# Splitting a weight into hi and lo parts ahead of time and keeping both in DRAM: the second block's mixers

## The chip, the cores and the metric

The kernel runs on one core of a Trainium2 chip. A core has a matrix engine (PE in the profile), three engines for elementwise work (DVE is VectorE, ACT is ScalarE, POOL is GpSimd), a queue engine (SP) that issues this kernel's transfers, and 16 DMA engines that carry them between DRAM and the on-chip memory SBUF. Matrix products are summed in PSUM banks of 128 x 512 float32. The metric is the device time of one execution in microseconds; lower is better. Before the change the median of three runs is 2828.16 us (2825.42 to 2829.25).

## The reference, cut to what matters

Two transformer blocks run one after the other on 512 tokens (528 with 16 extra tokens in front in the first block), with model width 1024, all in float32.

- Block one has two hybrid layers. Each projects the normalized activations with `w_in`, runs three attentions (one with a forget gate, one with low-rank queries and keys, one with a sliding window), and ends with `merged = sum(sigmoid(gates) * (branches @ w_branch))` and `x + merged @ w_out`.
- Block two has two layers, each a mixer, an MLP `square(relu(h @ w_mlp_in)) @ w_mlp_out`, and a gated addition. Layer 0's mixer is `mixer_ab`: `h @ w_in_ab` feeds four differential-attention heads and eight dilated-attention heads, and their outputs are multiplied by `w_out_ab`. Layer 1's mixer is `mixer_c`: `h @ w_in_c` gives low-rank queries, keys and an index score; the 256 best keys of each query are selected; `w_qi`, `w_uq`, `w_uk`, `w_uv` make queries, keys and values, and `w_out_c` closes it.

The products must be close to float32 products. That is why every weight `w` and activation `a` is split in two: `w = hi + lo`, `a = hi + lo`.

## The kernel before, in words

Activations are held transposed, 128 channels to a tile and tokens along the free axis. Weights lie in DRAM in chunks of 128 output columns, each chunk `[128, kc, 128]` with `kc` groups of 128 input channels. A projection of one chunk (`proj`) is, for each of the `kc` groups, three matmuls into one PSUM bank: hi x hi, hi x lo, lo x hi.

`wload` brings a chunk in. It cuts it into pieces of 512 columns (four groups, at most 256 KB). For each piece SP issues a load into a raw tile (tag `wraw`, a ring of 4), ACT copies the raw tile to `wh` (line 383, this rounds it), and DVE or POOL subtracts to make `wl` (line 385). `wh` and `wl` are rings of 3 each, so a piece's buffers come free when PE has finished the matmuls of the piece three before. The engine of the subtraction goes round DVE, POOL, DVE (`weng`, counted by `wn`); while `mixer_c` selects its keys, `weng` holds POOL alone.

The order of work on each engine is set by a planner that simulates the program and places instructions by its own estimates of time; each engine and the SP queue then run their own list strictly in that order, so an instruction that waits holds up all that is queued behind it.

The stages that the change touches, in order of time:

- The end of a hybrid layer. A first loop over eight output chunks (`for oc in range(8)`, from `gate(2, oc, 1)`) loads three pieces for a gate and a branch and makes the merged activations. A second loop loads the two pieces of `wout`, and its consumer (lines 1177 to 1180 for layer 0, 1189 to 1192 for layer 1) loads a residual tile `xc` from DRAM, adds the product, stores it (`x1d` or `h2d`), and splits it for the next stage. Each layer's end has 16 iterations in all. The query tiles `s.qt` of the attentions (four hi/lo pairs) are no longer used there.
- `mixer_ab`, lines 1401 to 1531. Each of eight pairs of heads needs three chunks of `wab` (two pieces each, 48 pieces in all); a pair's rotary step sends four small transfers through SP (line 832). `out_part` with `woab` runs in three parts over the input channels (groups 0 to 3, 4 to 6, and 7), eight pieces in each, of four, three and one group: 24 pieces.
- The first MLP, `mlp` with `l = 0`: two halves of 16 input chunks (two pieces each) and eight output chunks (four pieces each).
- `mixer_c`, lines 1533 to 1746: `wc` has 14 pieces, `wqi` 8, `wuq2` 16, `wukv2` 8, and `woc` again 24: 70 pieces.

Of the kernel before, what the change touches and what calls it, by code (L numbers as in the profile page):

```python
# [10 lines left out]
F32 = mybir.dt.float32  # L11
F32R = mybir.dt.float32r
# [8 lines left out]
P = 128  # L21
KC = 8
NM = 16
NX = 512
# [7 lines left out]
RINGT = dict(tmp=4, mm=6, sm=2)  # L32
PLE1 = 4
AHEAD = 4
OUTK = 4, 7
MLA_SCALE = 96 ** -0.5
LAM_INIT = 0.8 - 0.6 * math.exp(-0.0)
# [250 lines left out]
class Kern:  # L288
    def __init__(s, ctx, tc, a, out):
        s.ctx, s.tc, s.nc, s.a, s.out = ctx, tc, tc.nc, a, out  # L290
        s.n = s.wn = 0
        s.weng = [tc.nc.vector, tc.nc.gpsimd, tc.nc.vector]

    def nm(s, x):
        s.n += 1
# [73 lines left out]
    def wload(s, src, pool=None):  # L369
        kc, n = src.shape[1], src.shape[2]  # L370
        nc = s.nc
        step = max(1, 512 // n)
        hs, ls = [], []
        for k0 in range(0, kc, step):
            m = min(step, kc - k0)
            raw = s.wp.tile([P, m, n], F32, tag="wraw", bufs=4, name=s.nm("wr"))
            nc.sync.dma_start(raw, src[:, k0:k0 + m])
            if pool is None:
                h = s.wp.tile([P, m, n], F32R, tag="wh", bufs=3, name=s.nm("wh"))
                l = s.wp.tile([P, m, n], F32R, tag="wl", bufs=3, name=s.nm("wl"))  # L380
            else:
                h, l = (pool.tile([P, NX], F32R, tag=x, name=s.nm(x)).rearrange("p (m n) -> p m n", m=m) for x in ("fh", "fl"))
            nc.scalar.copy(h, raw)  # L383
            s.wn += 1
            s.weng[s.wn % len(s.weng)].tensor_sub(l, raw, h.bitcast(F32))  # L385
            for k in range(m):
                hs.append(h[:, k])
                ls.append(l[:, k])
        return hs, ls

    def proj(s, w, acts, toks, c0=0, m=P, k0=0, tag="mm"):
# [447 lines left out]
    def hybrid(s, l, acts, rc, meta):  # L839

        nc, c = s.nc, s.c
# [5 lines left out]
        rstd = s.spread(rc, NT)  # L847
        win = s.a[f"win{l}"]
        W = lambda name: s.first.pop(name, None) or s.wload(win[WIN_IDX[name]])
        with ExitStack() as sc:  # L850
# [42 lines left out]
            for ps, t0, n in s.proj(W("misc"), acts, allt, tag="pv"):  # L893
# [3 lines left out]
            cq, rq = s.lora_raw([lambda i=i: s.proj(W(f"cq{i}"), acts, allt) for i in range(3)], f"cq{l}", ytile,  # L897
                                s.acc1(), NT, rc)
# [5 lines left out]
            for t0, n in allt:  # L904
                ps = s.bank("ax", "kf")
# [27 lines left out]
            ys = [[], [], []]  # L933
# [168 lines left out]
                       + [(swa, swa_do, swa_more, p) for p in range(4)])  # L1102
            yc = [ysplit(y) for y in ys[2]]
            mhl = []
            for oc in range(8):
                t = gate(2, oc, 1)
                branch(2, oc, yc, t, t)
                m = mg[oc]
                nc.gpsimd.tensor_add(m[:, c0:NT], m[:, c0:NT], t[:, c0:NT])
                h = s.yp.tile([P, NT], F32R, tag="y", name=s.nm("mh"))  # L1110
                lo = s.yp.tile([P, NT], F32R, tag="y", name=s.nm("ml"))
                nc.scalar.activation(h[:, c0:NT], m[:, c0:NT], AF.Copy, scale=0.5)
                nc.vector.scalar_tensor_tensor(lo[:, c0:NT], m[:, c0:NT], 0.5, h[:, c0:NT].bitcast(F32),
                                               op0=OP.mult, op1=OP.subtract)
                mhl.append((h, lo))

            for oc in range(8):
                w = s.wload(s.a[f"wout{l}"][oc])
                yield oc, s.proj(w, mhl, qt)

# [156 lines left out]
    def out_part(s, wname, acts, k0, k1, ys, tag=None, bufs=None):  # L1277

        acc = s.new_acc() if k1 == KC else None
        for oc in range(KC):  # L1280
            (ps, _, _), = s.proj(s.wload(s.a[wname][oc, :, k0:k1]), acts[k0:k1], [(0, NX)])
            if k0 == 0:
                y = s.t512(tag, bufs)
                s.nc.scalar.copy(y, ps)
                ys.append(y)
            else:
                s.nc.vector.tensor_add(ys[oc], ys[oc], ps)
            if k1 == KC:
                s.square_acc(ys[oc], acc, NX, oc == 0, oc == KC - 1)
        return ys, acc  # L1290
# [14 lines left out]
            s.nc.scalar.activation(t, ps, AF.Copy, scale=0.5)  # L1305
            s.pp.append(t)

    def mlp(s, l, acts, rstd, fp, w):
        nc = s.nc
        ys = []  # L1310
        acc = s.new_acc()
        r2 = s.tp.tile([P, NT], F32, tag="rstd", bufs=2, name=s.nm("r2"))
        nc.gpsimd.tensor_mul(r2[:, :NX], rstd[:, :NX], rstd[:, :NX])
        for half in range(2):
            ff = []
            for fc in range(16):
                (ps, _, _), = s.proj(w.pop(0) if w else s.wload(s.a[f"wmi{l}"][16 * half + fc]), acts, [(0, NX)])
                f = s.tmp("ff")[:, :NX]
                nc.vector.tensor_scalar(f, ps, 0.0, None, op0=OP.max)  # L1319
                nc.gpsimd.tensor_mul(f, f, f)  # L1320
                fh = fp.tile([P, NX], F32R, tag="fh", name=s.nm("fh"))
                fl = fp.tile([P, NX], F32R, tag="fl", name=s.nm("fl"))
                nc.scalar.copy(fh, f)
                nc.vector.tensor_sub(fl, f, fh.bitcast(F32))
                ff.append((fh, fl))
            for oc in range(KC):
                (ps, _, _), = s.proj(s.wload(s.a[f"wmo{l}"][oc, :, 16 * half:16 * half + 16]), ff, [(0, NX)])
                if half == 0:
                    y = s.t512("s", 16)
                    nc.scalar.copy(y, ps)  # L1330
                    ys.append(y)
                else:
                    y = ys[oc]
                    nc.vector.tensor_add(y, y, ps)
                    (nc.vector if oc == KC - 1 else nc.gpsimd).tensor_mul(y, y, r2[:, :NX])
                    s.square_acc(y, acc, NX, oc == 0, oc >= KC - 2)
        return ys, acc
# [19 lines left out]
    def tail_layer(s, l, ys, acc):  # L1357

        with ExitStack() as ps:
            s.rings(ps, **RINGT)  # L1360
            s.pp = []
            s.ple_proj(l, range(0, PLE1))
            with s.tc.tile_pool(name=f"ff{l}", bufs=16) as fp, s.tc.tile_pool(name=f"pe{l}", bufs=1) as pep:

                w = []
                acts, acc = s.post(ys, acc, f"mpost{l}", f"fpre{l}", lambda: w.extend(
                    s.wload(s.a[f"wmi{l}"][fc], fp) for fc in range(AHEAD)))
                rstd = s.rstd_of(acc, NX, 1024)
                s.ple_load(l, lambda: pep.tile([P, NX], F32R, name=s.nm("p")))
                ys, acc = s.mlp(l, acts, rstd, fp, w)  # L1370
                s.ple_proj(l, range(PLE1, KC))
            acts, _ = s.post(ys, acc, f"fpost{l}", None)
            sums = s.new_acc() if l == 0 else None
            s.ple_gate(l, acts, sums)
            return sums
# [25 lines left out]
    def mixer_ab(s, acts, rstd, load):  # L1401
# [4 lines left out]
        with ExitStack() as sc:  # L1406
# [21 lines left out]

            def scaled(ch, scale=1.0):
                v = s.tmp("v")  # L1430
                (ps, _, _), = s.proj(s.wload(s.a["wab"][ch]), acts, tk)
                nc.vector.scalar_tensor_tensor(v[:, :NX], ps, scale, rstd[:, :NX], op0=OP.mult, op1=OP.mult)  # L1432
                return v

# [98 lines left out]
    def mixer_c(s, acts, rc):  # L1533
# [4 lines left out]
        with ExitStack() as sc:  # L1538
# [6 lines left out]
            def raw(ch, n):  # L1545
                res = []
                for i in range(n):
                    v = s.t512("s", 16)
                    (ps, _, _), = s.proj(s.wload(s.a["wc"][ch + i]), acts, tk)
                    nc.vector.tensor_mul(v, ps, rstd[:, :NX])  # L1550
                    res.append(v)
                return res
# [4 lines left out]
            def lora(raw, gname):  # L1557
# [5 lines left out]
                for i, v in enumerate(raw):  # L1563
# [4 lines left out]
                    res.append((h, lo))  # L1568
                return res

            cq, rq = s.lora_raw([lambda i=i: s.proj(s.wload(s.a["wc"][2 + i]), acts, tk) for i in range(3)], "cq2", ctile,
                                s.new_acc(), NX, rc)

            (ps, _, _), = s.proj(s.wload(s.a["wc"][0]), acts, tk)
            s.table("kit", 0)
            s.table("qit", 1)
            foldki, selki = s.cld("foldki", kp), s.cld("selki", kp)
            kr = s.tmp("kr")[:, :NX]
            nc.vector.tensor_mul(kr, ps, rstd[:, :NX])
            nc.vector.tensor_mul(kr, kr, c["kit"][:, :NX])  # L1580
            (ps, _, _), = s.proj(s.wload(s.a["wc"][1]), acts, tk)
            m2 = s.tmp("m2")[:, :NX]
            nc.vector.tensor_mul(m2[0:64], ps[0:64], rstd[0:64, :NX])
            ps = s.bank("ax", "kf")
# [20 lines left out]
            score = [s.ap.tile([P, NX], F32, tag="Ph", bufs=3, name=s.nm("sc")) for _ in range(3)]  # L1605
            qi = []
            for h in range(8):
                (ps, _, _), = s.proj(s.wload(s.a["wqi"][h]), cq, [(P, 384)])
                q = s.tmp("qi")
                nc.vector.tensor_mul(q[:, P:NX], ps[:, :384], c["qit"][:, P:NX])  # L1610
                qh, ql = s.t512("s", 16, F32R), s.t512("s", 16, F32R)
                s.split(q[:, :NX], qh, ql, slice(P, NX), nc.vector if h % 2 else nc.gpsimd)
                qi.append((qh, ql))
# [20 lines left out]
            def query(i):  # L1634


                h, k = i & ~3, i & 3
                (ps, _, _), = s.proj(s.wload(s.a["wuq2"][i]), cq, tk)
                v = s.tmp("q")[:, :NX]
                if k < 2:  # L1640
                    for _ in range(2):
# [28 lines left out]
            outs = []  # L1670

            def mla(p):
                wkv = s.wload(s.a["wukv2"][p])
                v = s.tmp("v")
                (ps, _, _), = s.proj(wkv, ckv, tk, c0=P)
                nc.scalar.copy(v[:, :NX], ps)
# [88 lines left out]
```

## Time and profile before

| what | value |
|---|---|
| median of three runs | 2828.16 us |
| the profiled execution's own time | 2830.3 us |
| its span, first to last instruction | 2828.5 us |
| PE busy | 2708.7 us (96%) |
| DVE busy | 1629.7 us (58%) |
| ACT busy | 1225.3 us (43%) |
| POOL busy | 1186.1 us (42%) |
| mean granted TensorE clock | 0.978 of full speed |
| transfers on the SP queue | 249.43 MB, 29.5% of the 16 DMA engines' span |

The shares are averages over the whole span. PE is nearly always busy, but the profile's busy time counts a slowed matmul as fully busy, so the granted clock must be read beside it. What an engine's work is worth has to be read from its stage: DVE's share in particular is far from even over the span.

### The profile page before, as it was taken

To read this page: it belongs to the slowest core of one execution; us is meant where nothing else is said; L and a number is where in the kernel's file an instruction comes from. 1 tells how busy PE (TensorE), PEld (TensorE's weight loads), DVE (VectorE), ACT (ScalarE), POOL (GpSimd) and SP (SyncE) were. 2 spreads that over 40 slices of the span, in tenths; PEclk is the share of its full clock that TensorE was granted. 3 is DMA by queue.
4 is the path that set the end of the run, shared out by engine and by line. 5 is a ranking of instruction groups with operands and counts; after the bars stand their busy time and mean duration, and the time that the engine had idled before them with its cause. 6 is when DMAs were issued, how large, how long until landed. Compare 5 with 4: busy or idle time off the path is not lost. (4 is left out here: it accounts for less than half of the span.)

```text
span 2828.5 us, 41363 instructions
## 1 busy us (share of the span) xinstructions
PE 2708.7 (96%) x14962; PEld 2306.3 (82%) x14962; DVE 1629.7 (58%) x2997; ACT 1225.3 (43%) x2267; POOL 1186.1 (42%) x1091
## 2 busy tenths in 40 slices
PE   8999999999999999999988999999998898999998
PEld 7999999999888887877766768888776776788886
DVE  5666666644576667545688863132459876522325
ACT  4554444433454444434455543232344665322323
POOL 3455445432334334346455452133336434422333
PEclk9999999999999999999999999999999998999999
DMA  4222232234322233325322223333233212233322
GB/s 144 65 67 80 76 96 84 79 102 136 99 70 76 68 90 98 94 94 185 105 74 76 67 87 97 93 96 94 75 92 92 75 35 63 83 94 96 94 86 89
DMA packets 146669, 252.08 MB, mean 89 GB/s; under 512 B 19680, under 2 KB 32864, under 8 KB 146464
## 3 DMA queue, kind: packets, MB, share of 16 engines
q1 hardware_dynamic: 146464, 249.43, 29.5%
q8 instruction: 118, 1.93, 0.3%
q14 instruction: 87, 0.71, 0.1%
HBM read 215.26 MB, written 6.42 MB: 78 GB/s over the span
## 5 line engine op out<-in xcount | busy, mean ns | idle before, releaser
L383 ACT CAST wh<-wr 128x512 fp32r<-128x512 f32 (+3 forms) x774 | 463.8, 601 | 987.8 <-PE mm L362 815.8
L362 PE MATMUL mm<-xh,wh 128*128 128x264 f32 (+2 forms) x2464 | 849.4, 347 | 28.3 <-ACT xh L1141 8.2
L362 PE MATMUL mm<-xl,wh 128*128 128x264 f32 (+1 forms) x2480 | 852.0, 345 | 5.1 <-DVE xl L1142 1.7
L362 PE MATMUL mm<-xh,wl 128*128 128x264 f32 (+2 forms) x2464 | 845.4, 344 | 2.0 <-DVE wl L385 1.3
L385 POOL TENSOR_TENSOR wl<-wr,wh 128x512 fp32r<-128x512 f32 (+2 forms) x273 | 350.1, 1283 | 804.1 <-ACT wh L383 792.9
L385 DVE TENSOR_TENSOR wl<-wr,wh 128x512 fp32r<-128x512 f32 (+3 forms) x501 | 383.6, 766 | 398.6 <-ACT wh L383 389.9
L362 PEld LDWEIGHTS mm<-xh,wh 128*128 128x128 f32 x2464 | 469.8, 191 | 90.7 <-DVE v L1432 8.3
L362 PEld LDWEIGHTS mm<-xl,wh 128*128 128x128 f32 x2480 | 473.6, 191 | 62.2 <-DVE xl L1142 2.9
L362 PEld LDWEIGHTS mm<-xh,wl 128*128 128x128 f32 x2464 | 469.3, 191 | 58.9 <-DVE wl L385 3.2
L564 POOL TENSOR_TENSOR Pl<-P,Ph 128x512 fp32r<-128x512 f32 (+4 forms) x108 | 131.5, 1218 | 169.0 <-ACT P L563 144.9
L362 PE MATMUL mm<-fh,wl 128*128 128x512 f32 x512 | 202.3, 395 | 0.0
L362 PE MATMUL mm<-fl,wh 128*128 128x512 f32 x512 | 202.0, 395 | 0.0
L362 PE MATMUL mm<-fh,wh 128*128 128x512 f32 x512 | 202.0, 395 | 0.0
L563 ACT ACTIVATE Ph<-st 128x512 fp32r<-128x512 f32 (+4 forms) x224 | 122.1, 545 | 128.1 <-PE st L362 79.9
L564 DVE TENSOR_TENSOR Pl<-P,Ph 128x512 fp32r<-128x512 f32 (+4 forms) x108 | 83.1, 769 | 123.6 <-ACT P L563 110.7
L362 PE MATMUL mm<-c,wh 128*128 128x264 f32 (+2 forms) x480 | 127.9, 353 | 9.5 <-ACT q L1645 4.7
L1320 POOL TENSOR_TENSOR ff<-ff 128x512 f32<-128x512 f32 x64 | 82.2, 1286 | 106.3 <-DVE ff L1319 106.3
L701 DVE RECIPROCAL zr<-zr 128x128 f32<-128x128 f32 (+1 forms) x144 | 123.2, 916 | 2.7 <-ACT zr L710 2.4
L563 ACT ACTIVATE P<-st 128x512 f32<-128x512 f32 (+4 forms) x216 | 116.8, 541 | 6.5 <-POOL Pl L564 3.0
L483 POOL TENSOR_TENSOR acc<-acc,sq 128x512 f32<-128x512 f32 (+1 forms) x64 | 92.0, 1442 | 60.6 <-ACT sq L479 54.8
L362 PEld LDWEIGHTS mm<-fl,wh 128*128 128x128 f32 x512 | 96.5, 188 | 22.5
L362 PEld LDWEIGHTS mm<-fh,wl 128*128 128x128 f32 x512 | 96.5, 188 | 22.3
(612 smaller groups left out, 5154.2 us busy)
## 6 DMA issues: line engine op xcount, KB each, us to landing
wr<-in_win_dram SPq DMA_DIRECT2D x240, 256.0 KB
wr<-in_wmi_dram SPq DMA_DIRECT2D x128, 256.0 KB
wr<-in_wmo_dram SPq DMA_DIRECT2D x128, 256.0 KB
wr<-in_wbr_dram SPq DMA_DIRECT2D x48, 256.0 KB
wr<-in_wab_dram SPq DMA_DIRECT2D x48, 256.0 KB
wr<-in_wout_dram SPq DMA_DIRECT2D x32, 256.0 KB
wr<-in_wpg_dram SPq DMA_DIRECT2D x32, 256.0 KB
wr<-in_wuq_dram SPq DMA_DIRECT2D x32, 192.0 KB
```

The costliest lines, as they stand in the source:

```text
L362: s.nc.tensor.matmul(out, l, r, start=start, stop=stop)
L383: nc.scalar.copy(h, raw)
L385: s.weng[s.wn % len(s.weng)].tensor_sub(l, raw, h.bitcast(F32))
L483: e[eng[1]].tensor_add(sums.t[:, :T], sums.t[:, :T], q[:, :T])
L563: nc.scalar.activation(o[:, :col], ps[:, :col], AF.Exp)
L564: s.pl_eng(ui, hn).tensor_sub(pl[:, :col], p[:, :col], ph[:, :col].bitcast(F32))
L701: s.nc.vector.reciprocal(t[:, a:b], t[:, a:b])
L1320: nc.gpsimd.tensor_mul(f, f, f)
```

## The change

`pieces` lists a weight's pieces as keys. `ahead` takes the next keys from a list `todo`; for each it loads the raw piece, copies it to a hi tile, subtracts to a lo tile, and stores both tiles to a DRAM tile `d` of `[128, 2, w]`. `wget` takes the place of `wload` in the mixers: where a piece is found in `pre`, it loads hi and lo straight into `wh` and `wl` (two transfers, no ACT copy and no subtraction); otherwise it falls back to `wload`.

```diff
+AHEADN = (2, 2), (3, 2), (1, 3)
...
+    def ahead(s, count, tiles):
+        nc = s.nc
+        for _ in range(min(count, len(s.todo))):
+            key = name, ch, k0, m = s.todo.pop(0)
+            w = m * s.a[name].shape[3]
+            raw = s.wp.tile([P, m, w // m], F32, tag="wraw", bufs=4, name=s.nm("wr"))
+            nc.sync.dma_start(raw, s.a[name][ch, :, k0:k0 + m])
+            raw = raw.rearrange("p m n -> p (m n)")
+            d = s.dp.tile([P, 2, w], F32R, name=s.nm("wd"))
+            h, l = (t[:, :w] for t in tiles())
+            nc.scalar.copy(h, raw)
+            s.wn += 1
+            s.weng[s.wn % len(s.weng)].tensor_sub(l, raw, h.bitcast(F32))
+            s.rdma(d[:, 0], h)
+            s.rdma(d[:, 1], l)
+            s.pre[key] = d
+
+    def wget(s, name, ch, k0=0, k1=None):
+        hs, ls = [], []
+        for key in s.pieces(name, ch, k0, k1):
+            _, _, k, m = key
+            d = s.pre.get(key)
+            if d is None:
+                h, l = s.wload(s.a[name][ch, :, k:k + m])
...
+            h = s.wp.tile([P, m, n], F32R, tag="wh", bufs=3, name=s.nm("wh"))
+            l = s.wp.tile([P, m, n], F32R, tag="wl", bufs=3, name=s.nm("wl"))
+            for t, i in ((h, 0), (l, 1)):
+                s.rdma(t.rearrange("p m n -> p (m n)"), d[:, i])
...
             for oc in range(8):
+                s.ahead(AHEADN[l][0], tiles)
                 t = gate(2, oc, 1)
...
             for oc in range(8):
+                s.ahead(AHEADN[l][1], tiles)
                 w = s.wload(s.a[f"wout{l}"][oc])
...
             for fc in range(16):
+                if not w:
+                    later(AHEADN[2][0])
...
             for oc in range(KC):
+                later(AHEADN[2][1])
...
-                (ps, _, _), = s.proj(s.wload(s.a["wab"][ch]), acts, tk)
+                (ps, _, _), = s.proj(s.wget("wab", ch), acts, tk)
```

The same replacement of `wload` by `wget` is made for `woab` and `woc` (in `out_part`), `wc`, `wqi`, `wuq2` and `wukv2`. In the hybrid layers `tiles` hands out the four pairs of `s.qt` in turn; in the first MLP `later` uses a new pool with two hi and two lo tiles.

What is prepared where follows from the counts. The first `todo` (48 pieces of `wab`, 24 of `woab`) is used up in the two hybrid ends: 2 in each of 16 iterations of layer 0 (32 pieces), 3 and then 2 in each of eight iterations of layer 1 (40 pieces). The second (70 pieces) is used up in the first MLP: 1 in each of 28 input chunks, 3 in each output chunk.

## Rows read from the trace of the kernel before

**Rows 1.** The page: busy time of PE, and the granted clock in 40 slices.
```profile
PE 2708.7 (96%) x14962; PEld 2306.3 (82%) x14962; DVE 1629.7 (58%) x2997; ACT 1225.3 (43%) x2267; POOL 1186.1 (42%) x1091
...
PEclk9999999999999999999999999999999998999999
```

**Rows 2.** Stretches: stretch, length, busy us (instructions) of five engines, clock, DMA share, GB/s.
```profile
563.00:632.00 69.00, 67.25 (x550) 66.96 (x550) 32.55 (x59) 24.33 (x40) 26.52 (x18) 1.00 0.31 97
632.00:682.00 50.00, 50.00 (x414) 49.96 (x413) 22.70 (x38) 22.09 (x35) 18.16 (x13) 1.00 0.52 166
1205.00:1272.00 67.00, 67.00 (x290) 54.03 (x289) 30.82 (x43) 23.75 (x40) 26.42 (x20) 1.00 0.32 99
1272.00:1318.00 46.00, 46.00 (x216) 37.80 (x215) 20.41 (x34) 25.40 (x43) 31.54 (x35) 1.00 0.60 187
1340.00:1626.00 286.00, 255.84 (x1141) 196.99 (x1139) 233.17 (x396) 148.96 (x275) 146.56 (x120) 0.95 0.29 81
1672.00:2012.00 340.00, 340.00 (x1472) 275.21 (x1471) 102.00 (x150) 100.30 (x171) 108.28 (x84) 1.00 0.30 92
2075.00:2205.00 130.00, 114.05 (x517) 92.72 (x517) 102.49 (x231) 58.01 (x112) 66.36 (x56) 0.93 0.34 94
```

**Rows 3.** Waits of PE, 1318 to 1680 us: total us, times, longest.
```profile
PE mm L362 <- DVE v L1432: 5.9, 6, 1.5
PE st L362 <- DVE rz L1495: 4.9, 3, 2.8
...
PE zs L1479 <- POOL zacc L569: 3.6, 3, 1.6
...
PE sm L362 <- DVE ng L514: 2.7, 3, 1.4
```

**Rows 4.** Groups by line, 1340 to 1626 us: the weight split's three engines.
```profile
L385 DVE TENSOR_TENSOR wl<-wr,wh 128x512 fp32r<-128x512 f32 (+3 forms) x43 | 38.8, 903 | 4.1 <-ACT wh L383 3.8
L383 ACT CAST wh<-wr 128x512 fp32r<-128x512 f32 (+3 forms) x64 | 35.1, 555 | 40.2 <-PE mm L362 29.5 <-issue 8.3 <-ACT y L711 1.4
L385 POOL TENSOR_TENSOR wl<-wr,wh 128x512 fp32r<-128x512 f32 (+3 forms) x22 | 28.0, 1274 | 18.6 <-ACT wh L383 18.6
```

**Rows 5.** One line, 1340 to 1626 us: min/median/max ns.
```profile
L836 DVE TENSOR_TENSOR v<-v,sw x15: 674/1181/1778, 1341.9 to 1566.1; 128x512 f32<-128x512 f32 x15
```

**Rows 6.** A short stretch of the first mixer, columns as in rows 2.
```profile
1550.00:1556.00 6.00, 2.73 (x10) 1.59 (x9) 6.00 (x12) 4.19 (x8) 4.63 (x3) 0.73 0.22 72
```

**Rows 7.** The chain that ended last: start, us, what.
```profile
1545.78 1.97 DMA sw<-v
...
1572.76 2.77 PE mm L362 x12
...
1626.15 5.79 PE mm L362 x24
...
1636.79 2.71 DMA wr<-in_wmi_dram
...
2118.55 1.56 PE mm L362 x9
```

**Rows 8.** SP's queue in layer 0's last loop: start, us, instruction.
```profile
650.28 0.38 SPq L1180 DMA_DIRECT2D x1d<-xc  x1
650.71 0.42 SPq L1177 DMA_DIRECT2D xc<-in_xt_dram  x1
...
655.78 0.33 SPq L1180 DMA_DIRECT2D x1d<-xc  x1
```

**Rows 9.** The stretch with the highest transfer rate, columns as in rows 2.
```profile
10.00:14.00 4.00, 4.00 (x22) 3.79 (x20) 3.61 (x5) 4.00 (x8) 2.67 (x2) 1.00 1.05 402
```

**Rows 10.** The second mixer's key selection, columns as in rows 2.
```profile
2140.00:2145.00 5.00, 5.00 (x23) 4.05 (x22) 5.00 (x13) 2.24 (x5) 1.02 (x1) 1.00 0.07 25
2180.00:2185.00 5.00, 0.55 (x3) 0.13 (x1) 5.00 (x16) 0.51 (x1) 5.00 (x5) 0.93 0.38 89
```

**Rows 11.** POOL's groups by shape, 2100 to 2215 us.
```profile
L385 POOL TENSOR_TENSOR wl<-wr,wh 128x384 fp32r<-128x384 f32 x19 | 20.1, 1062 | 34.9 <-ACT wh L383 34.9
L385 POOL TENSOR_TENSOR wl<-wr,wh 128x512 fp32r<-128x512 f32 x6 | 7.9, 1314 | 4.8 <-ACT wh L383 4.8
```

More of the change, by code (lines that the diff above doesn't have):

```diff
@@ L292, in __init__ @@
         s.weng = [tc.nc.vector, tc.nc.gpsimd, tc.nc.vector]
+        s.pre, s.todo = {}, []
     def nm(s, x):
@@ L388, in wload, with pieces @@
                 ls.append(l[:, k])
+        return hs, ls
+    def pieces(s, name, ch, k0=0, k1=None):
+        kc, n = s.a[name].shape[2], s.a[name].shape[3]
+        k1 = kc if k1 is None else k1
+        step = max(1, 512 // n)
+        return [(name, ch, k, min(step, k1 - k)) for k in range(k0, k1, step)]
+    def ahead(s, count, tiles):
[21 more added lines that the diff above has]
+                h, l = s.wload(s.a[name][ch, :, k:k + m])
+                hs += h
+                ls += l
+                continue
+            n = s.a[name].shape[3]
+            h = s.wp.tile([P, m, n], F32R, tag="wh", bufs=3, name=s.nm("wh"))
+            l = s.wp.tile([P, m, n], F32R, tag="wl", bufs=3, name=s.nm("wl"))
+            for t, i in ((h, 0), (l, 1)):
+                s.rdma(t.rearrange("p m n -> p (m n)"), d[:, i])
+            for i in range(m):
+                hs.append(h[:, i])
+                ls.append(l[:, i])
         return hs, ls
@@ L1104, in hybrid, with tiles @@
             mhl = []
+            if l == 0:
+                s.todo = sum((s.pieces("wab", b + p) for b, q in ((0, 8), (12, 20)) for p in range(4)
+                              for b in ((q, b + 4, b))), [])
+                s.todo += sum((s.pieces("woab", oc, *r) for r in ((0, OUTK[0]), OUTK, (OUTK[1], KC)) for oc in range(8)), [])
+            turn = [0]
+            def tiles():
+                turn[0] += 1
+                return s.qt[turn[0] % len(s.qt)]
             for oc in range(8):
+                s.ahead(AHEADN[l][0], tiles)
                 t = gate(2, oc, 1)
@@ L1280, in out_part @@
         for oc in range(KC):
-            (ps, _, _), = s.proj(s.wload(s.a[wname][oc, :, k0:k1]), acts[k0:k1], [(0, NX)])
+            (ps, _, _), = s.proj(s.wget(wname, oc, k0, k1), acts[k0:k1], [(0, NX)])
             if k0 == 0:
@@ L1306, in ple_proj, with mlp, later @@
             s.pp.append(t)
-    def mlp(s, l, acts, rstd, fp, w):
+    def mlp(s, l, acts, rstd, fp, w, spare=None):
         nc = s.nc
         ys = []
+        if l == 0:
+            s.todo = sum((s.pieces("wc", ch) for ch in (2, 3, 4, 0, 1)), [])
+            for name, n in (("wqi", range(8)), ("wc", (5, 6)), ("wuq2", range(16)), ("wukv2", range(8))):
+                s.todo += sum((s.pieces(name, ch) for ch in n), [])
+            s.todo += sum((s.pieces("woc", oc, *r) for r in ((0, OUTK[0]), OUTK, (OUTK[1], KC)) for oc in range(8)), [])
+        def later(n):
+            if l == 0:
+                s.ahead(n, lambda: [spare.tile([P, NX], F32R, tag=x, bufs=2, name=s.nm(x)) for x in ("sh", "sl")])
         acc = s.new_acc()
@@ L1369, in tail_layer @@
                 s.ple_load(l, lambda: pep.tile([P, NX], F32R, name=s.nm("p")))
-                ys, acc = s.mlp(l, acts, rstd, fp, w)
+                with s.tc.tile_pool(name=f"sp{l}", bufs=1) as spare:
+                    ys, acc = s.mlp(l, acts, rstd, fp, w, spare)
                 s.ple_proj(l, range(PLE1, KC))
@@ L1548, in raw @@
                     v = s.t512("s", 16)
-                    (ps, _, _), = s.proj(s.wload(s.a["wc"][ch + i]), acts, tk)
+                    (ps, _, _), = s.proj(s.wget("wc", ch + i), acts, tk)
                     nc.vector.tensor_mul(v, ps, rstd[:, :NX])
@@ L1569, in lora @@
                 return res
-            cq, rq = s.lora_raw([lambda i=i: s.proj(s.wload(s.a["wc"][2 + i]), acts, tk) for i in range(3)], "cq2", ctile,
+            cq, rq = s.lora_raw([lambda i=i: s.proj(s.wget("wc", 2 + i), acts, tk) for i in range(3)], "cq2", ctile,
                                 s.new_acc(), NX, rc)
-            (ps, _, _), = s.proj(s.wload(s.a["wc"][0]), acts, tk)
+            (ps, _, _), = s.proj(s.wget("wc", 0), acts, tk)
             s.table("kit", 0)
@@ L1580, in mixer_c @@
             nc.vector.tensor_mul(kr, kr, c["kit"][:, :NX])
-            (ps, _, _), = s.proj(s.wload(s.a["wc"][1]), acts, tk)
+            (ps, _, _), = s.proj(s.wget("wc", 1), acts, tk)
             m2 = s.tmp("m2")[:, :NX]
@@ L1607, in mixer_c @@
             for h in range(8):
-                (ps, _, _), = s.proj(s.wload(s.a["wqi"][h]), cq, [(P, 384)])
+                (ps, _, _), = s.proj(s.wget("wqi", h), cq, [(P, 384)])
                 q = s.tmp("qi")
@@ L1637, in query @@
                 h, k = i & ~3, i & 3
-                (ps, _, _), = s.proj(s.wload(s.a["wuq2"][i]), cq, tk)
+                (ps, _, _), = s.proj(s.wget("wuq2", i), cq, tk)
                 v = s.tmp("q")[:, :NX]
@@ L1672, in mla @@
             def mla(p):
-                wkv = s.wload(s.a["wukv2"][p])
+                wkv = s.wget("wukv2", p)
                 v = s.tmp("v")
```

## The prediction, made before the changed kernel was run

> **What bounds the kernel now.** I read the page first, then a table of stretches by stage, then who PE waits for in the stretches that the change touches, and last the groups, the chain and the SP queue there. The page says that PE is busy 96% and its clock nearly full everywhere [rows 1], so this is a PE-bound kernel and an edit that takes work from other engines can only earn what PE idles or loses to its clock. Where that is shows in the stretches [rows 2]. The two hybrid ends (563 to 682 and 1205 to 1318 us) and the first MLP (1672 to 2012) have PE full, or all but 2 us of it, at clock 1.00: nothing can be won there, only lost. In the first mixer (1340 to 1626) PE is busy 255.84 of 286 us at clock 0.95, while DVE is busy 233.17, 82%. In the second mixer's first part (2075 to 2205) PE is busy 114.05 of 130.
>
> **What the change can win: first mixer.** Its ceiling is 286 - 255.84 = 30 us of idle PE, and (1 - 0.95) x 286 = 14 us of slow clock: 44 us. The clock belongs to the idle time: when PE was busy only 2.73 of 6 us with DVE full, the granted clock of that stretch fell to 0.73 [rows 6], between the levels of 2.4 and 1.2 GHz. The change takes from this stretch 43 DVE subtractions, 38.8 us, 22 on POOL, 28.0 us, and 64 ACT copies, 35.1 us [rows 4]; a few belong to the loads behind the mixer and stay. DVE falls to about 195 us, 68%. Its own slowed operations should gain too: one DVE addition took from 674 to 1778 ns at the same shape [rows 5], but I count nothing for that, since I can't say how many slow ones sit beside a subtraction that goes.
>
> How much of the 44 us comes back? PE's largest waits there are for DVE and POOL, 5.9 + 4.9 + 3.6 + 2.7 = 17.1 us [rows 3], and almost none is for a split weight itself. So what can be won is the queue in front of other DVE and POOL work. What is late next is the chain through a pair of heads: evacuation, rotary transfers, maxima, exponentials. I take 40% of the ceiling, 18 us: some 12 of idle time, two thirds of the named waits, and 6 of clock. Bounds: nothing (the chain is as long as before) and 36 us (80%).
>
> **What the mixers pay: loads that come late.** Before, a piece needs an ACT copy and a subtraction once its buffer is free: 0.55 + 0.90 us at the means on DVE, more with queues [rows 4]. Now SP must issue two loads when PE frees the buffer, at 0.33 to 0.42 us each [rows 8], and they land after 1.97 us (a small one) to 2.71 us (256 KB) [rows 7]: about 3.5 us. PE takes 2.77 us for twelve matmuls of a 512-column piece [rows 7], so two pieces in hand cover 5.5 us, and `wqi`'s pieces, 1.56 us each plus score matmuls [rows 7], cover a little over 3. Hidden, then, but with the cover thin, and the loads share SP with the rotary transfers: I put 1 us for it, from 0 to 8.
>
> The one-group pieces at the end of `woab` and `woc` have no such cover. Eight of them are 24 matmuls in 5.79 us, 0.72 each [rows 7]. Of the first three the loads go out while PE is still on larger pieces. The next three wait: free at 0.72, landed some 2.7 us later, done at about 5.6; the last two again, done near 8.3. That is 2.5 us more at each of the two mixer ends, on PE's path: 5 us, from 0 (casts and additions there are as slow) to 10.
>
> **Second mixer.** POOL loses 25 subtractions, 20.1 + 7.9 us [rows 11], in a stretch where it runs full at times. But DVE, which selects the keys, is full from 2140 on, also where PE has nearly nothing to do [rows 10], and subtractions there are POOL's already, so the end of the selection hardly moves. I take 3 us won, from 4 lost (the plan there changes) to 8 of the 16 us that PE idles.
>
> **What is added where PE is full.** The elementwise work first. In layer 0's last loop ACT, DVE and POOL are busy 22, 23 and 18 of 50 us [rows 2]; 16 copies and 16 subtractions at the means of rows 4 add 9 us to ACT and 14 to DVE, or 20 if all fell on POOL. It fits; cover gone, each would cost PE at most its length. The first MLP has a third of each engine busy in 340 us, and 70 pieces add 39 us to ACT and 63 to 89 us of subtractions: 0, at most 6 if copies wait for the two spare tiles.
>
> The transfers don't fit as well. A 256 KB piece now moves three times in these stages, read once and written twice: 0.786 MB. Layer 0's last loop takes 16 pieces, 12.6 MB, on top of 166 GB/s x 50 us = 8.3 MB: 418 GB/s would be wanted. The best that the trace shows is 402 [rows 9], so this loop is 2 us too short for its bytes. Layer 1's first loop takes 24 pieces on 99 GB/s: 381 GB/s; its last one 8 of 192 KB and 8 of 64 KB on 187 GB/s: 324; layer 0's first loop 279; the MLP's output half, 24 pieces of mostly 192 KB in about 88 us on 92 GB/s, some 265. The Trainium skill's page "HBM Reference", section "Specifications (TRN2)", gives an effective 358 GB/s per core, which speaks against this change; its text also lets a core that streams alone go well above that. Rows 9 have such a core at 402, so the measurement decides; by 358 the two stretches above it would be 8 and 4 us too short.
>
> Latency is the other half. In these loops SP stores a result, loads the next residual tile at 650.71, and the store that needs it follows at 655.78: 5.1 us in a period of 5.5 [rows 8]. Six more issues per iteration stand in this queue (2 raw loads, 4 stores that wait for copies and subtractions), 2 to 2.5 us at 0.33 to 0.42, and each raw load of a main weight and each residual tile waits behind up to 1.5 MB. Behind a waiting store stand the main weights; the rings hold some 8 us of those, PE's banks of results about one half-chunk. I take 5 us for layer 0 and 2 for layer 1, together 7, from 0 to 32 (2 us in each of 16 iterations).
>
> **Sum.** On the profiled execution's 2830.3 us, 2.1 above the median: -18 + 1 + 5 - 3 + 0 + 7 = -8, so 2822.3, and against the median of 2828.2 about 2820.
>
> **The rivals.**
> *The hybrid ends become bound by transfers.* From the point at which residual tiles and main weights land later than PE's banks allow, the loop's period is SP's and the queue's, not PE's. For it: 418 GB/s wanted where 402 was the best, and the 5.1 of 5.5 us. Against: weights run far ahead, and the other stretches stay below 402. The page named above belongs to this rival. Price: 1.75 us more in 16 iterations, 28 instead of 7: 2841.
> *The first mixer doesn't shorten.* The time per pair of heads is set by its chain, not by DVE's load, or the win goes to weights that wait behind rotary transfers. For it: waits for split weights were near nothing, and ring depth falls to three. Against: DVE at 82% with PE's waits naming it. Price: 7 won instead of 18, and the rest as above: 2831, near enough to no change.
> *The change doesn't do what it says.* All 72 and 70 pieces find their turn by the counts, so nothing falls back to the old path; I give it no chance of its own.
>
> **How the numbers follow.** Forecast 0.45, transfers bound 0.29, mixer unshortened 0.26. A measurement of this kernel can't tell less than 0.2%, 5.7 us, from no change. The forecast's own range is 2806 to 2824, so a little of it is no change, and the second rival reaches a bit to both sides: faster 0.46, same 0.24, slower 0.30. The time is the forecast's, 2820; the range takes both rivals in, 2798 to 2844.
>
> **What would show it.** After the change the first mixer's stretch should have no subtraction of mixer weights, DVE near 70%, and be 13 to 20 us shorter, with fewer low-clock stretches. PE should wait for loaded `wh` or `wl` in the one-group ends, some 2.5 us each, and hardly elsewhere. The hybrid ends should show 300 to 400 GB/s and PE idle a few us in layer 0's last loop. I am wrong if PE idles there by 20 us, if the first mixer is as long as before, or if the first MLP is no longer full.

## The result: 2.2% slower

The changed kernel takes 2890.0 us (median of 4 runs, 2878.41 to 2901.93) against 2827.2 us for the kernel before: ratio 1.0222, 95% interval [1.0202, 1.0241], or 63 us more. The forecast was 2820 and the range ended at 2844.

The page of the changed kernel: busy time, clock, the SP queue and the bytes.
```profile
PE 2728.3 (95%) x14962; PEld 2292.0 (80%) x14962; DVE 1650.8 (57%) x3012; ACT 1224.2 (43%) x2267; POOL 1167.0 (41%) x1076
...
PEclk9999999999999999999999999999999999999999
...
q1 hardware_dynamic: 228256, 375.30, 42.0%
...
HBM read 278.17 MB, written 69.34 MB: 121 GB/s over the span
```
Against [rows 1] PE does the same 14962 matmuls and its share falls. The SP queue carries 126 MB more, half of it stores. The profiled execution is the fastest of the four (2878.4 us, clock 0.984; the other three had 0.978 to 0.980), so the stages below add up to 48 of the 63 us.

The stretches that answer to [rows 2], in the same order: stretch, length, busy us (instructions) of five engines, clock, DMA share, GB/s. Each is shifted and stretched by its own landmarks.
```profile
565.00:635.00 70.00, 65.72 (x520) 64.48 (x519) 35.51 (x59) 29.52 (x52) 27.87 (x21) 0.99 0.76 254
635.00:698.00 63.00, 57.11 (x426) 55.09 (x425) 31.03 (x50) 28.74 (x48) 23.14 (x17) 0.95 0.93 311
1223.00:1305.00 82.00, 72.88 (x290) 53.44 (x289) 45.54 (x60) 36.09 (x62) 35.55 (x27) 0.98 0.83 278
1305.00:1361.50 56.50, 50.11 (x219) 37.42 (x218) 26.14 (x39) 26.36 (x51) 34.25 (x38) 1.00 0.80 249
1383.50:1654.00 270.50, 251.15 (x1141) 194.19 (x1139) 201.13 (x354) 118.52 (x214) 117.59 (x99) 0.97 0.47 140
1700.00:2068.00 368.00, 350.17 (x1455) 268.38 (x1454) 139.39 (x195) 129.13 (x236) 133.44 (x107) 1.00 0.61 196
2131.00:2261.00 130.00, 118.28 (x545) 95.46 (x545) 92.88 (x220) 43.21 (x82) 39.55 (x32) 0.97 0.55 163
```
The first mixer, fifth row, does its 1141 matmuls in 270.5 instead of 286 us, at a higher clock: the win is there. The MLP, sixth row, had PE full for 340 us; now about the same matmuls take 368 us and PE idles 18. In the four rows of the hybrid ends PE idled 2 us in all before, and now 4 to 9 us in each.

How much each stage grew in one profiled execution of each kernel, from landmark instructions: the last `x1d` store (679.2 us before), the last matmul on `mh` (1309.0), the MLP's first matmul (1640.8), the first matmul of `m` with `selki` in the second mixer (2113.3), the last store of the output (2825.9). The other columns are experiments described below. Stages that a kernel leaves alone differ by up to 5.4 us here, and by nearly 8 in two other runs, so smaller differences are not read.

| stage, us against before | changed | reads only | no stores | narrow stores | narrow, ready | full, ready | late stores |
|---|---|---|---|---|---|---|---|
| up to layer 0's end | +16.0 | -4.2 | +8.8 | +12.7 | +8.4 | +17.6 | +12.3 |
| layer 1, its end | +27.5 | +0.2 | +10.4 | +22.3 | +14.1 | +18.4 | +17.6 |
| first mixer | -15.4 | -16.5 | +4.2 | +3.4 | +4.2 | +3.8 | -13.2 |
| first MLP | +27.9 | -0.4 | -2.0 | +18.2 | -0.8 | +12.4 | +20.3 |
| second mixer and rest | -7.9 | +0.2 | +5.0 | +5.4 | +0.9 | +4.8 | -4.2 |

What ends the waits in the MLP, 1740 to 2090 us: first SP's queue (total us, times, longest), then ACT. L1195 is a store of a prepared half, L380 a main weight's raw load, L407 a raw load ahead.
```profile
SPq L1195 <- ACT sh L411: 116.9, 50, 5.2
SPq L380 <- POOL wl L388: 37.2, 17, 4.5
SPq L380 <- DVE wl L388: 20.7, 14, 2.8
```
```profile
ACT sh L411 <- DMA wr<-in_woc_dram: 39.8, 20, 3.6
...
ACT sh L411 <- DMA wr<-in_wuq_dram: 36.5, 15, 4.1
ACT wh L386 <- DMA wr<-in_wmo_dram: 31.3, 22, 3.6
ACT sh L411 <- DMA wr<-in_wukv_dram: 20.7, 8, 4.6
```
For 117 of 350 us SP stands at a store whose hi half ACT has not copied yet. ACT in turn waits for that piece to land, and then 31 us for main weights to land. In the kernel before ACT waited for the opposite thing, for PE to give buffers back (same view, 1720 to 2060 us):
```profile
ACT wh L383 <- PE mm L362: 154.4, 77, 2.9
```
SP's queue then waited for raw buffers alone:
```profile
SPq L377 <- DVE wl L385: 156.1, 76, 3.9
SPq L377 <- POOL wl L385: 135.6, 40, 15.6
```
So weights used to run ahead of PE and now arrive behind it. The chain of waits in the changed MLP shows how one wait leads to the next (start, us, what; pieces of 0.05 us and less are left out):
```profile
1765.70 4.34 DMA wr<-in_wqi_dram
1770.12 0.52 ACT sh L411
1770.64 0.07 issue
1770.71 1.03 POOL sl L413
1771.76 0.33 SPq L1195
1772.14 0.42 SPq L407
1772.66 3.99 DMA wr<-in_wmo_dram
1776.73 0.63 ACT wh L386
```
A piece lands, is copied and subtracted, its second store goes out, and only then the loads behind it are issued; the main weight among them lands 3.99 us later, where a load of that size took 2.71 us [rows 7]. PE is not in these rows at all.

### The profile page after: what moved, and what is told of

Its sections match the earlier page's. It is cut to its first block, busy times and chain, and to the rows that moved or that the text cites. A ratio compares the mean times of both kernels' runs of the same rounds, so it can differ in the third digit from the quotient of the medians.

```text
span 2876.6 us, 42388 instructions
## 1 busy us (share of the span) xinstructions
PE 2728.3 (95%) x14962; PEld 2292.0 (80%) x14962; DVE 1650.8 (57%) x3012; ACT 1224.2 (43%) x2267; POOL 1167.0 (41%) x1076
## 4 chain that ended last, share of the span: by engine, by line
PE 49%; DMA 10%; DVE 9%; ACT 3%; issue 3%; POOL 2%; SPq 1%; ACTq 0%; DVEq 0%; POOLq 0%
PE mm L365 40%; PE st L365 3%; PE pv L365 3%; DMA wr<-in_wab_dram 1%; DMA wr<-in_wuq_dram 1%; DMA wr<-in_wmo_dram 1%; DVE h L1333 1%; PE sm L365 1%; DVE wl L388 1%; DMA wr<-in_wukv_dram 1%; DMA wr<-in_woc_dram 1%; DMA wr<-in_win_dram 1%; POOL wl L388 1%; ACT wh L386 1%; DMA wl<-wd 1%
## 5 line engine op out<-in xcount | busy, mean ns | idle before, releaser
L386 ACT CAST wh<-wr 128x512 fp32r<-128x512 f32 (+2 forms) x632 | 384.7, 611 | 695.4 <-PE mm L365 496.4
L388 POOL TENSOR_TENSOR wl<-wr,wh 128x512 fp32r<-128x512 f32 (+2 forms) x220 | 289.3, 1315 | 649.5 <-ACT wh L386 623.0
L388 DVE TENSOR_TENSOR wl<-wr,wh 128x512 fp32r<-128x512 f32 (+2 forms) x412 | 328.4, 798 | 339.8 <-ACT wh L386 329.5
L365 PEld LDWEIGHTS mm<-fh,wh 128*128 128x128 f32 x512 | 96.4, 188 | 32.7 <-ACT wh L386 11.7
```

The source lines that it names most:

```text
L365: s.nc.tensor.matmul(out, l, r, start=start, stop=stop)
```

## The experiments

Two theories stood at the start. *Waiting theory*: SP works its list in order, and stores that wait for ACT hold up the main weights' loads. *Byte theory*: the transfers fill the DMA engines. Times are medians against the kernel before on the same chip; us are (ratio - 1) x 2828.

**The mixers' win alone.** Three pieces are prepared in layer 0's end and all mixers read them over and over, so the output is not the reference's; nothing else is prepared.
```diff
-AHEADN = (2, 2), (3, 2), (1, 3)
+AHEADN = (3, 0), (0, 0), (0, 0)
...
-            s.pre[key] = d
+            s.pre[w] = d
...
-            d = s.pre.get(key)
+            d = s.pre.get(m * s.a[name].shape[3])
...
```


> Three pieces (one of each width) are prepared in layer 0's end; every mixer piece then loads these three from DRAM, so the mixers run the changed path and nothing else is prepared (the weights of the mixers are wrong, the output is not the reference's). All theories of what the preparation costs agree here: only the mixers' side is left, which the trace of the changed kernel puts at 15 us won in the first mixer and 8 in the second: 2804 us, between 2796 and 2812. Rival: the mixers won in the changed kernel only because PE came to them late with loads already made; then no win, 2820 to 2830.

Measured: 2807.37, ratio 0.9927 [0.9904, 0.9949], 21 us faster. In the table, 16.5 of it is the first mixer; of the 8 expected in the second, nothing shows. So the preparation costs the changed kernel 63 + 21 = 84 us.

**Loads, copies and subtractions, but no stores.** The mixers split their own weights again.
```diff
-            s.rdma(d[:, 0], h)
-            s.rdma(d[:, 1], l)
-            s.pre[key] = d
```


> All 142 pieces are still loaded and split ahead, but not stored; the mixers load and split their weights as before the change (the work ahead is thrown away). Queue theory (the stores stand in SP's strict order behind copies and subtractions, and main loads stand behind them): the cost goes, 2827 to 2840 us. Bytes theory (the DMA engines are full): two thirds of the added bytes go, 2827 to 2845. Engine theory (copies and subtractions delay the main weights' own): the cost of 71 us in stretches where PE was full stays, 2885 to 2900.

Measured: 2857.41, ratio 1.0097 [1.007, 1.0124], 27 us: between what the queue and byte theories expected and what the engine theory did, so none of them holds alone. The MLP costs nothing here; the layers' ends do. The stores cost the other 84 - 27 = 57.

**Stores of 64 columns**, about a seventh of the stored bytes (284 stores of 32 KB); mixers as before.
```diff
-            s.rdma(d[:, 0], h)
-            s.rdma(d[:, 1], l)
-            s.pre[key] = d
+            s.rdma(d[:, 0, :64], h[:, :64])
+            s.rdma(d[:, 1, :64], l[:, :64])
```


> As the run without stores, but each store is still issued, with 64 of its up to 512 columns; mixers as before the change. Queue theory: the same issues wait for the same copies, so most of the 71 us stays, 2875 to 2900 us. Bytes theory: as without stores, 2827 to 2850. Engine theory: 2885 to 2900.

Measured: 2888.64, ratio 1.0216 [1.0188, 1.0244], 61 us. With a seventh of the stored bytes, 34 us more than without stores: bytes alone fall as the explanation.

**The same narrow stores, from a constant that is always ready**, issued behind the piece's own load; mixers as before, and the pieces are not kept.
```diff
+            with s.tc.issue_after(ld.ins):
+                for i in range(2):
+                    nc.sync.dma_start(d[:, i, :64].bitcast(F32), s.ones[:, :64])
...
-            s.rdma(d[:, 0], h)
-            s.rdma(d[:, 1], l)
-            s.pre[key] = d
```


> As the run with small stores (two per piece, 64 columns), but the stores read a constant that is ready from the start and stand right behind their piece's load in SP's queue, so they never wait for a copy or a subtraction; what they store is not the weights, and the mixers split their weights themselves as before. Waiting theory (SP stands at a store until its copy is made, and main loads stand behind): the 31 us between the runs without stores and with small ones go, 2850 to 2865 us. Issue theory (284 more issues at 0.33 us and more fill SP's time): they stay, 2880 to 2897.

Measured: 2857.83, ratio 1.0102 [1.0087, 1.0117], 29 us, as without stores. Issuing and moving narrow stores costs nothing that these runs resolve; waiting for their data costs 61 - 29 = 32. (A store with its own data also keeps its tile until it has gone out, but ACT has no wait for a tile to be given back by a store in the MLP, neither with narrow stores nor in the changed kernel.) SP's waits in the MLP, narrow stores with their own data (1740 to 2090 us):
```profile
SPq L1194 <- ACT sh L411: 127.3, 54, 5.6
```
and from the constant (1740 to 2080 us), where no store is left among the long waits and SP waits for free raw buffers, as a queue does that runs ahead:
```profile
SPq L380 <- POOL wl L388: 61.1, 29, 4.9
SPq L380 <- DVE wl L388: 51.9, 27, 17.5
```

**Ready stores of full width**, from a constant tile; nothing waits, all bytes move, the pieces are not kept.
```diff
+            with s.tc.issue_after(ld.ins):
+                for i in range(2):
+                    nc.sync.dma_start(d[:, i].bitcast(F32).rearrange("p (m n) -> p m n", n=c), s.rdy[:, :c].unsqueeze(1).to_broadcast([P, w // c, c]))
```


> The kernel whose 64-column stores came from a tile that is always ready took 2857.8, as much as without stores. Here the stores from such a ready tile have the changed kernel's full width, so they wait for nothing but move all its bytes (what they store is not the pieces, and the mixers split their own weights as before). If the store bytes cost the remaining 23 us of the changed kernel's preparation (2890 less the 21 won in the mixers' favour against 60 us with narrow stores), it takes about 2875 to 2885. If bytes cost nothing once nobody waits for the store, it takes 2855 to 2862.

Measured: 2884.95, ratio 1.0197 [1.0179, 1.0215], 56 us: the bytes are worth 56 - 29 = 27. (By the edit these stores go out in smaller rows, of at most 1 KB where the changed kernel's have up to 2 KB; the next run moves the changed kernel's own stores and comes to the same.) The MLP with narrow and with full ready stores, columns as above:
```profile
1695.00:2036.00 341.00, 341.00 (x1470) 275.81 (x1469) 138.61 (x199) 130.99 (x237) 138.22 (x110) 1.00 0.48 144
```
```profile
1708.00:2064.00 356.00, 350.50 (x1486) 275.63 (x1485) 137.25 (x199) 131.58 (x240) 137.95 (x110) 1.00 0.66 204
```
The same elementwise work is hidden completely at 144 GB/s. At 204 GB/s PE idles 5.5 us and the stage is 15 us longer, though the DMA engines are busy only 0.66.

**Stores later in the queue.** The changed kernel, but a piece's stores go behind the second main load after it.
```diff
             ld = nc.sync.dma_start(raw, src[:, k0:k0 + m])
+            s.mains += 1
+            if s.held and s.mains - s.held[0][0] >= 2:
+                with s.tc.issue_after(ld.ins):
+                    s.flush(1)
...
-            s.rdma(d[:, 0], h)
-            s.rdma(d[:, 1], l)
+            s.held.append((s.mains, d, h, l))
```


> The changed kernel with each pair of stores queued on SP behind the second main load after its piece, so that the copy is mostly made when SP gets there. Waiting theory: of the 83 us that the preparation costs (2890 against 2807 with the mixers' side alone) about 31 go, 2850 to 2868 us. Bytes theory: nothing changes, 2878 to 2900. Issue theory: nothing changes either.

Measured: 2864.32, ratio 1.0128 [1.0111, 1.0145], 36 us. With the mixers' 21 added back, the preparation costs 57, just what the full ready stores cost (56). SP's store waits in the MLP fell from 116.9 to
```profile
SPq L1205 <- ACT sh L421: 19.4, 15, 3.0
```
so in the whole kernel the waits were a cost, not a sign of it. In the MLP itself the table falls less, from +27.9 to +20.3. There ACT now stands at another wait (1690 to 2060 us), for a late store to give back one of the two spare tiles:
```profile
ACT sh L421 <- DMA wd<-sh: 28.7, 14, 4.0
```
What more spare tiles would give was not tried.

**Late stores, and raw tiles of their own in the layers' ends.**
```diff
-            raw = s.wp.tile([P, m, w // m], F32, tag="wraw", bufs=4, name=s.nm("wr"))
+            raw = own[0][:, :w].rearrange("p (m n) -> p m n", m=m)
```


> The run with late stores, and in the hybrid ends the raw pieces that are split ahead use four idle tiles of their own instead of the ring of four that the main loads use. Ring theory (the main loads run fewer pieces ahead because the ring is shared): of the 19 us that loads and splits alone cost in the two ends some 12 to 19 go, so 12 to 19 us below the run with late stores alone, 2833 to 2853 us. Bytes or engine theory: same as with late stores.

Measured: 2857.7, ratio 1.0118 [1.0081, 1.0155]. Not told apart from the late stores alone (one of its four runs took 2878.5, the others 2855 to 2859). The same tiles without stores:

> The run without stores, with raw tiles of their own in the hybrid ends; mixers as before, the work ahead is thrown away. Ring theory: from 2857 down to 2832 to 2845 us, the two ends together at most 7 us longer than before. Engine theory (copies and subtractions in the way of the main weights' own) or bytes theory (one third of the added bytes is still read): 2852 to 2862.

Measured: 2857.88, ratio 1.0103 [1.0088, 1.0118], as with the shared ring (2857.41). That loads ahead take raw buffers from the main weights is not what the 27 us are.

**Stores from POOL's queue** in the changed kernel.
```diff
-            s.rdma(d[:, 0], h)
-            s.rdma(d[:, 1], l)
+            nc.gpsimd.dma_start(d[:, 0].bitcast(F32), h.bitcast(F32))
+            nc.gpsimd.dma_start(d[:, 1].bitcast(F32), l.bitcast(F32))
```


> The changed kernel with its stores issued from POOL's queue instead of SP's; all bytes, all work the same. Queue theory: the main loads no longer stand behind stores, so most of the 71 us goes and the mixers' 23 us stay won: 2805 to 2840 us. Bytes theory: as the changed kernel, 2875 to 2900. Engine theory: 2875 to 2900, or more, since POOL now waits too.

Measured: 2947.03, ratio 1.0416 [1.0395, 1.0437], 118 us: worse by 55 than from SP, a clear miss of what was expected. The wait changes its place: POOL now stands at the stores, and the main weights' subtractions in its list behind them. POOL's waits, 560 to 2140 us, and its instructions at the same line:
```profile
POOL wd L414 <- ACT sh L411: 111.3, 38, 5.3
```
```profile
L414 POOL DMA_DIRECT2D wd<-sh x70: 540/559/582, 1717.5 to 2089.7; - x70
```
Besides, each store takes POOL itself 0.56 us, some 159 us for 284. How the 55 us divide between the waits and this work was not separated.

**The remaining 27 us, halved.** First the copies and subtractions alone, on a tile that is always ready, at the place of a main weight's copy; no loads ahead, no stores, mixers as before.
```diff
-            nc.sync.dma_start(raw, s.a[name][ch, :, k0:k0 + m])
+            raw = s.rdy[:, :c].unsqueeze(1).to_broadcast([P, w // c, c])
...
-            nc.scalar.copy(h, raw)
+            with s.tc.issue_after(s.cast.ins):
+                nc.scalar.copy(h.rearrange("p (m n) -> p m n", n=c), raw)
```


> The changed kernel's ACT copies and subtractions alone: each prepared piece is copied and subtracted from a tile that is always ready, in the same places and number; no raw load ahead, no store, and the mixers split their own weights as before. The kernel with loads and splits but no stores took 2857.4, 29 us over the kernel before. If those 29 us are the work of the copies and subtractions on ACT, DVE and POOL (engine theory), this kernel takes about 2850 to 2860. If they are ACT standing, in order, at a copy whose piece has not landed, with the main weights' copies behind it (load theory), it takes about 2828 to 2838. If they are the bytes of the loads on the DMA engines (byte theory), also 2828 to 2838; the next kernel tells these two apart.

Measured: 2842.67, ratio 1.0052 [1.0034, 1.0069], 15 us. Then the loads ahead alone, which nothing reads:
```diff
-            nc.scalar.copy(h, raw)
-            s.wn += 1
-            s.weng[s.wn % len(s.weng)].tensor_sub(l, raw, h.bitcast(F32))
```


> The changed kernel's raw loads alone: the pieces are loaded into the four raw tiles by SyncE in the same places and nothing reads them; no copy, no subtraction, no store, and the mixers split their own weights as before. Engine theory and load theory (ACT standing at a copy) both expect the time of the kernel before, about 2825 to 2835. Byte theory expects the 29 us here: 2850 to 2860.

Measured: 2841.62, ratio 1.0052 [1.0037, 1.0067], 15 us. Each is about half of the 27, and both lie between what the theories expected: none has all of it. The loads show in layer 0's end, 560 to 710 us, where the residual tile that stands behind them in SP's list comes late. Before, and with loads only:
```profile
DVE xc L1179 <- DMA xc<-in_xt_dram: 10.5, 4, 3.1
```
```profile
DVE xc L1231 <- DMA xc<-in_xt_dram: 24.4, 6, 7.3
```
By the landmarks above the stages that were changed are only 4.2 (copies and subtractions) and 3.1 us (loads) longer, of 9.8 and 10.8 in these two executions. The first mixer, whose code is the same here, is 2.6 and 7.5 us longer, and it is longer, by 2.6 to 7.7, in all seven kernels whose mixers split their own weights. So where these 27 us are paid stays open; whether the planner's changed order has a part in them was not tested.

**Half as many pieces**, stores late as above; 76 of the 142 pieces are prepared by the count of their stores, and the rest is split by the mixers.
```diff
-AHEADN = (2, 2), (3, 2), (1, 3)
+AHEADN = (1, 1), (1, 1), (1, 1)
```


> The changed kernel with one piece prepared per step everywhere in place of two, three and one-to-three, and with the stores of a piece queued behind the second main load after it; what is not prepared in time the mixers split as before, so the output is complete. At the full rate with the same late stores the time was 2864, 36 us over the kernel before, of which the mixers gave back some 21. If the cost goes with the number of pieces, about half of 57 us is paid in the two layers' ends and two thirds in the MLP, some 33 us, and some 13 are won back: 2840 to 2855. If the cost is that of the worst stretches alone (three pieces in a step), the rest is nearly free and it takes 2815 to 2828.

Measured: 2848.8, ratio 1.0075 [1.0054, 1.0096], 21 us. With late stores a piece costs 57 / 142 = 0.40 us and gives back 21 / 142 = 0.15 us. For 76 pieces that makes 19 us lost, and 21 were. The cost goes with the number of pieces, and on this line no rate above zero wins, so no version to beat both kernels follows from this. Preparing in other stages was not tried.

## Why the prediction was wrong

Two terms failed, both in the part on what is added where PE is full: +7 for the hybrid ends, where 43.5 us were paid, and 0 for the first MLP, where 27.9 were. Over the whole kernel the runs name three costs behind them: SP's wait at a store, 32 us, which the prediction held to at most 2 us per iteration in the ends, took at 7 in all, and left out in the MLP; the stored bytes, 27 us, which it compared with 402 GB/s; and the loads and splits themselves, 27 to 29 us, where it put the splits at 0. The term for the first mixer was right.

- **First mixer, -18: right.** -15.4 in the changed kernel, -16.5 with the reads alone. PE's idle time there fell from 30.2 to 19.4 us and the clock rose from 0.95 to 0.97; DVE is at 74%, where about 70 was expected. In PE's waits, 1352 to 1710 us, the addition in DVE's queue stays (5.9 us [rows 3]), and `zacc` fell from 3.6 us; the wait for `rz` (4.9 us) went to 0.3. Of the 17.1 us of named waits about half went, where two thirds were expected:
```profile
PE mm L365 <- DVE v L1506: 6.1, 6, 1.9
...
PE mm L365 <- DMA wh<-wd: 2.4, 3, 1.8
...
PE zs L1553 <- POOL zacc L617: 1.2, 2, 0.8
```
- **Late loads +1: small, as expected. One-group ends +5: they did not come.** The end of `woab` shows one load on the chain, before the seventh of the eight one-group pieces, and 24 matmuls further on:
```profile
1648.86 2.06 DMA wh<-wd
...
1654.19 5.78 PE mm L365 x24
```
These 24 are not those pieces, and neither are the 24 of [rows 7] that the prediction took for them: they are the projection that follows (`ple_proj`, four chunks of two groups). The eight pieces' own matmuls, from the first one's start to the last one's end, took 8.3 us before (from 1616.94) and take 7.6 now (from 1645.16). PE waits for loaded tiles 2.4 + 0.7 us in the whole first mixer. In the second mixer three waits for a loaded `wl` make 5.8 us, the longest 4.5.
- **Second mixer, -3:** -7.9 in one execution of the changed kernel, +0.2 with the reads alone: single executions don't tell the expected -3 from nothing.
- **Hybrid ends, +7, up to 32: the step that failed first.** They cost 16.0 and 27.5 us; 8.8 and 10.4 of that are there without stores. The prediction named what happened ("Behind a waiting store stand the main weights") and trusted that the rings would cover it. A store does not wait once per iteration for 2 us: it waits for a load to land, then for ACT and a subtraction (4.34, 0.52 and 1.03 us in the MLP's chain above, 5.9 together), and the next loads are queued behind it. PE's waits in layer 1's end, 1223 to 1361.5 us, are for split weights:
```profile
PE mm L365 <- ACT wh L386: 9.4, 13, 1.8
PE mm L365 <- POOL wl L388: 5.7, 8, 1.6
```
- **The limit of 402 GB/s was taken from too short a stretch.** [Rows 9] is 4 us long. In the 6 us before it, in the same kernel and with loads alone, the DMA engines are full at 311. Where pieces are read and written together, in layer 0's last loop of the changed kernel, they are full at 326 (before, then changed; columns as in [rows 2]):
```profile
4.00:10.00 6.00, 1.82 (x6) 1.51 (x7) 2.61 (x3) 3.84 (x7) 1.36 (x2) 1.00 0.98 311
```
```profile
645.00:695.00 50.00, 44.11 (x331) 42.09 (x330) 23.50 (x38) 23.02 (x38) 18.84 (x14) 0.97 0.97 326
```
So no run shows that mixing reads and writes lowers the limit. [Rows 2] allowed a nearer estimate of it: rate over share is 166 / 0.52 = 319 GB/s in this loop before the change and 187 / 0.60 = 312 in layer 1's. By 326 the loop's 20.9 MB need 64 us and not 52; it took 63. But without stores the table shows nearly 9 of these 16 us already, so bandwidth is only part of it. The Trainium skill's page "HBM Reference", section "Specifications (TRN2)", gives 358 GB/s per core; the runs show 311 and 326 at a full share here, and the measurement decides.
- **First MLP, 0, up to 6: the largest miss, +27.9.** The elementwise work is hidden there, as forecast (-2.0 without stores). What was not priced is that the same waiting stores exist there, 140 of the 284: the transfers of the MLP were compared with the bandwidth alone, and their order in SP's list only in the hybrid ends. In the table, narrow stores cost 19 us more there with their own data than ready (+18.2 against -0.8), and ready stores 13 more at full width than narrow. With late stores 20.3 of the 27.9 stay, so how the MLP's share divides between waiting and bytes is not settled. The prediction's own sign of being wrong, "if the first MLP is no longer full", did appear. The Trainium skill's page "DMA: Bandwidth & Descriptors", section "Anatomy of one DMA — SWDGE (gpsimd) path", says that DMA engines never wait on semaphores, the issuing sequencer does. The narrow stores, 32 us dearer with their own data than from a constant, agree for SP's queue, and the 111.3 us of POOL's waits at its own stores for POOL's.
- **The rivals.** "The hybrid ends become bound by transfers" was the nearest and had the sign, but its place was one of three and its price, 28 for the ends, stood beside 43.5. "The first mixer doesn't shorten" fell: it shortened by 15.4.

By the medians: loads and splits 27 to 29, stores that wait 32, store bytes 27, less 21 won: 65 to 67, where 63 were measured. The first of these is measured, but its cause stays open.

## What to carry to other kernels

A transfer that waits for compute stops every load behind it in its issuing queue, so price a store by its wait (landing, copy, subtraction) and by what stands behind it, not by its bytes alone; put it late enough that its data is ready, or don't mix it with loads that feed the bounding engine. Spare average time is no cover when an engine at 100% lives on loads that run just ahead: the MLP had every helper two thirds idle and DMA at 0.30, and lost 28 us. Work moved out of a stage has to cost less where it goes than it gives back, per piece: here 0.40 against 0.15 us, with late stores.

## What the runs showed that was not expected

- Loads and stores together filled the DMA engines at 326 GB/s (share 0.97), loads alone at 311 (0.98); the 402 of [rows 9] held for 4 us only.
- At 204 GB/s and share 0.66 the MLP with ready stores already lost 15 us against the same at 144 GB/s: a mean share well under 1 does not say that loads land in time. A main weight's load took 3.99 us to land on the changed chain, 2.71 before.
- From POOL's queue the same stores cost 55 us more than from SP's, though SP's own list then held none of them.
